# Seven block products in place of eight for the feed-forward value chunks, and a down projection in three parts

## The chip, the cores and the metric

The kernel runs on one core of a Trainium2 chip. The metric is the device time of one execution in microseconds, the median of several runs. Five engines work at once, each through its own queue in the order in which the program wrote it: TensorE (PE, matrix products), VectorE (DVE), ScalarE (ACT), GpSimd (POOL) and SyncE (SP, which only starts transfers here). They wait for each other through semaphores.

## The reference, cut to what matters

Two blocks run one after the other on 512 tokens of width 1024. The first block has two layers, and each layer ends in the feed-forward part that is changed here:

```python
def conv_ffn(x, w_up, conv_w, conv_b, w_down):          # x: 512 x 1024, D_FF = 2816
    a, g = jnp.split(x @ w_up, 2, axis=-1)              # value half a, gate half g
    g = lax.conv_general_dilated(g, conv_w[:, None, :].astype(g.dtype), window_strides=(1,),
                                 padding=((CONV_W - 1, 0),), ..., feature_group_count=D_FF) + conv_b
    return (jax.nn.gelu(g) * a) @ w_down                # three-tap causal convolution per channel
```

The result is added to the residual and a layer norm follows. After the second layer an RMS norm for the next block follows as well.

## The kernel before, in words

All arithmetic is float32 to within rounding, by splitting. An operand is cut into a high part (a cast to the matmul's reduced format, on ACT, line 238 for weights and 371 for activations) and a low part (operand minus high part, on DVE at line 242 or POOL at 240, and 372). A product is then three matmuls: high x high, low x high, high x low (`mm3`, lines 276 to 278). The activations `xh`, `xl` lie transposed, 128 partitions x 8 slices of the width x 512 tokens.

The up projection works on chunks of 128 columns of D_FF, 22 gate chunks and 22 value chunks. A weight transfer (`unit`) of 1 MB brings the columns of two chunks into one of two `raw` buffers; each chunk is a `piece` that is split into a high and a low tile. `get` gives back the tiles of the piece just used and calls `pump`, which starts the next transfer if a `raw` buffer is free and issues the next split, up to five pieces ahead. So the splits of later pieces stand in ACT's and DVE's queues where `get` was called.

The order is two gate chunks, then the two value chunks that belong to them (a pair, 11 pairs in a layer). `fms` runs a chunk as 24 matmuls of 512 columns (8 slices x 3) into one PSUM bank (`fm`), then calls its evacuation. `g_evac` (line 1134) does the convolution and the gelu: ACT (1137), DVE twice (1138, 1139), ACT (1140). `a_evac` (1143) multiplies the value chunk from PSUM with the gate (DVE, 1145) and splits the product for the down projection. The first pair of a layer runs in two halves of 256 tokens (`split=SPL`), since the norm before it delivers the tokens in four tiles.

The chunks are taken in parts of 12 and 10 (`FF_PARTS`, line 1101). After each part the down projection (`tm`) multiplies its chunks with their rows of `w_down` in two halves of 512 output columns. The first part is added to the residual (`residual`, 405); the last goes through `out_proj`, whose last half works tile by tile of 128 tokens (`tail=5` pieces held at once), followed by each tile's layer norm (lines 403 to 425), the transposes (391) for the next stage, and in the second layer the RMS norm (443 to 451). `norm_params`, and in the second layer `lru_params` (some 30 very small DVE steps and an exponential on ACT), are issued after the first part's chunks.

Of the kernel before, what the change touches and what calls it, by code (L numbers as in the profile page):

```python
# [12 lines left out]
F32R = mybir.dt.float32r  # L13
# [15 lines left out]
SPL = 4  # L29
# [84 lines left out]
class Core:  # L114
# [4 lines left out]
    def __init__(self, ctx, tc, io):  # L119
# [17 lines left out]
        self.live = deque()  # L137
        self.nm = 0
# [37 lines left out]
    def piece(self, u, view, a, b, direct=False):  # L176
        self.units[u]["left"] += 1
        self.plist.append((u, view, a, b, direct))

    def pump(self, split=True):  # L180
        while True:
# [14 lines left out]
            if split and n < len(self.plist) and self.room():  # L196
                u, view, a, b, direct = self.plist[n]
                raw = self.units[u]["tile"]
                if raw is not None:
# [3 lines left out]
                    else:  # L203
                        self.live.append((None,) + self.split_piece(src, a, b))
                        self.units[u]["left"] -= 1
                    self.next_piece += 1
# [45 lines left out]
    held = 0  # L252

    def get(self, n=1):
# [11 lines left out]
        self.pump()  # L266
# [6 lines left out]
    def mm3(self, out, lhs, rhs, start, stop):  # L273
        (lh, ll), (rh, rl) = lhs, rhs
        mm = self.T.matmul
        mm(out, lh, rh, start=start, stop=False)  # L276
        mm(out, lh, rl, start=False, stop=False)  # L277
        mm(out, ll, rh, start=False, stop=stop)  # L278
# [12 lines left out]
    def fms(self, evacs, split=0):  # L291
# [3 lines left out]
        if split:  # L295
            self.flush(1)
            self.extra, self.eager = 0, False
            ws = self.get(split)
            pss = [self.ps() for _ in ws]
            for t0 in (0, 256):  # L300
                for k, (w, p) in enumerate(zip(ws, pss)):
                    if t0 or k == split - 1:
                        self.flush(3 if t0 else 2)
                    yield from self.fm(p, w, t0=t0, t1=t0 + 256)
                    if t0:
                        evacs[k](p)
                        if k == EAGER:
# [3 lines left out]
        for f in evacs[n:]:  # L311
# [3 lines left out]
            f(p)  # L315

# [784 lines left out]
    FF_PARTS = (12, 10)  # L1101

    def ffn_weights(self, l):
        w = self.io["ffn_w_up"][l].rearrange("(k p) n -> p k n", p=128)
        c = 0
        for part in self.FF_PARTS:
            for j in range(c, c + part, 2):
                for base in (D_FF, 0):
                    u = self.unit([(lambda r: r.rearrange("p (k n) -> p k n", k=8), w[:, :, base + 128 * j:base + 128 * j + 256])])
                    for q in range(2):  # L1110
# [16 lines left out]
    def ffn(self, l, rms=False):  # L1127
        A, V, al, fr = self.A, self.V, self.al, self.fr
# [14 lines left out]
        def a_evac(c, p):  # L1143
            acc = H[c]
            V.tensor_tensor(acc, p, acc, op=MUL)  # L1145
            hi, lo = al(F32R), al(F32R)
# [4 lines left out]
        for part in self.FF_PARTS:  # L1151
            fs = []
            for j in range(c0, c0 + part, 2):
                fs += [lambda p, c=c: g_evac(c, p) for c in (j, j + 1)] + [lambda p, c=c: a_evac(c, p) for c in (j, j + 1)]
            run(self.fms(fs, split=SPL if c0 == 0 else 0))
            if c0 == 0:
                gb = self.norm_params(l, 1)
                if rms:
# [977 lines left out]
```

## Time and profile before

| | us |
|---|---|
| time, median of 3 runs (2002.7 to 2004.19) | 2003.87 |
| the profiled execution's own time | 1997.43 |
| its span, first to last instruction | 1995.5 |
| PE busy with matmuls | 1947.4 (98%) |
| DVE busy | 991.2 (50%) |
| ACT busy | 817.5 (41%) |
| POOL busy | 417.6 (21%) |

All times in the rows are from the one profiled execution. Matmuls are pipelined: a matmul's own duration is longer than the distance to the next one, so their cost is read from the distance between two starts. The feed-forward part of the first layer starts at about 300 us and its last matmul is followed by the next stage's first at 665 us; the second layer's lies between about 964 and 1331 us.

### The profile page before, as it was taken

The numbers are of one execution on the slowest core, as the hardware profiler recorded it, in microseconds if no ns is written. First come the engines' busy times: TensorE is split into PE (matmuls) and PEld (weight loads), VectorE is DVE, ScalarE is ACT, GpSimd is POOL, SyncE is SP. The second block draws the span as 40 slices with busy tenths as digits, with TensorE's granted clock in tenths as the row PEclk, the third lists the DMA queues.
The fourth block names the chain that finished last, engine by engine and source line by source line (L and its number), as shares of the span: only waits on it lengthen the run. The fifth ranks groups of instructions, "written<-read, shape, count | busy, mean of one in ns | idle before, by whom it ended". The sixth has DMA issues, their size and how long they took to land.

```text
span 1995.5 us, 25737 instructions
## 1 busy us (share of the span) xinstructions
PE 1947.4 (98%) x10228; PEld 1623.8 (81%) x10228; DVE 991.2 (50%) x1692; ACT 817.5 (41%) x1451; POOL 417.6 (21%) x368
## 2 busy tenths in 40 slices
PE   8999989999999999999999999999998999999998
PEld 6678868888888988777888888888886888888887
DVE  3553255442444533763655344375667555455443
ACT  3455434331333344784333233256655533333331
POOL 0334441000000264474300000031443211011000
PEclk9999999999999999999999999999999999999999
DMA  6432223232323433111232423232231322222221
GB/s 199 112 115 68 93 84 101 95 127 85 105 85 123 137 99 122 54 49 64 65 116 94 137 85 105 85 106 70 71 89 70 133 85 90 90 85 90 85 75 52
DMA packets 174164, 189.22 MB, mean 95 GB/s; under 512 B 15080, under 2 KB 133662, under 8 KB 174045
## 3 DMA queue, kind: packets, MB, share of 16 engines
q1 hardware_dynamic: 158044, 165.63, 26.2%
q10 hardware_dynamic: 12064, 17.37, 2.9%
q0 software_dynamic: 3936, 4.59, 0.7%
q8 instruction: 80, 1.31, 0.3%
q14 instruction: 40, 0.32, 0.0%
HBM read 182.19 MB, written 6.65 MB: 95 GB/s over the span
## 4 chain that ended last, share of the span: by engine, by line
PE 80%; DVE 8%; ACT 3%; issue 2%; SPq 2%; DMA 2%; POOL 2%; ACTq 0%; DVEq 0%; POOLq 0%
PE p L276 24%; PE p L277 24%; PE p L278 24%; SPq L190 1%; PE p L1545 1%; PE p L1525 1%; PE p L1663 1%; SPq L851 1%; DVE s L1891 1%; POOL lo L240 1%; PE p L391 1%; PE p L786 1%; DVE s L1890 1%; PE p L366 1%; ACT hi L238 0%
## 5 line engine op out<-in xcount | busy, mean ns | idle before, releaser
L276 PE MATMUL p<-xh,hi 128*128 128x512 f32 (+1 forms) x1200 | 457.9, 382 | 0.7 <-ACT xh L371 0.7
L238 ACT CAST hi<-raw 128x1024 fp32r<-128x1024 f32 (+4 forms) x294 | 301.4, 1033 | 382.5 <-PE p L278 307.9
L277 PE MATMUL p<-xl,hi 128*128 128x512 f32 (+1 forms) x1200 | 454.3, 379 | 1.3 <-DVE xl L372 1.3
L278 PE MATMUL p<-xh,lo 128*128 128x512 f32 (+1 forms) x1200 | 454.3, 379 | 0.4 <-DVE lo L242 0.4
L242 DVE TENSOR_TENSOR lo<-raw,hi 128x1024 fp32r<-128x1024 f32 (+2 forms) x212 | 258.7, 1227 | 356.3 <-ACT hi L238 336.8
L276 PE MATMUL p<-hi,s 128*128 128x512 f32 (+1 forms) x728 | 285.7, 392 | 7.5 <-ACT s L371 4.8
L278 PE MATMUL p<-hi,s 128*128 128x512 f32 (+1 forms) x728 | 283.6, 390 | 0.0
L277 PE MATMUL p<-lo,s 128*128 128x512 f32 (+1 forms) x728 | 282.9, 389 | 0.0
L276 PEld LDWEIGHTS p<-xh,hi 128*128 128x128 f32 x1200 | 225.9, 188 | 44.7 <-ACT xh L371 1.4
L278 PEld LDWEIGHTS p<-xh,lo 128*128 128x128 f32 x1200 | 226.0, 188 | 43.1 <-DVE lo L242 0.6
L277 PEld LDWEIGHTS p<-xl,hi 128*128 128x128 f32 x1200 | 226.0, 188 | 42.8 <-DVE xl L372 2.1
L240 POOL TENSOR_TENSOR lo<-raw,hi 128x1024 fp32r<-128x1024 f32 (+3 forms) x82 | 191.2, 2339 | 329.2 <-ACT hi L238 259.6
L422 POOL TENSOR_TENSOR xtok<-xtok,b 128x512 f32<-128x512 f32 x16 | 26.1, 1629 | 712.9 <-ACT xtok L421 371.9
L276 PE MATMUL p<-hi,xh 128*128 128x512 f32 (+3 forms) x480 | 170.1, 354 | 1.5 <-ACT s L841 0.8
L277 PE MATMUL p<-lo,xh 128*128 128x512 f32 (+3 forms) x480 | 169.0, 352 | 0.5 <-DVE lo L242 0.5
L278 PE MATMUL p<-hi,xl 128*128 128x512 f32 (+3 forms) x480 | 168.8, 352 | 0.0
L276 PEld LDWEIGHTS p<-hi,s 128*128 128x128 f32 x728 | 137.1, 188 | 36.9 <-ACT s L371 6.2
L371 ACT CAST s<-s 128x512 fp32r<-128x512 f32 (+1 forms) x100 | 59.1, 597 | 260.8 <-DVE s L1145 122.7
L278 PEld LDWEIGHTS p<-hi,s 128*128 128x128 f32 x728 | 137.1, 188 | 30.0 <-DVE s L372 2.1
L277 PEld LDWEIGHTS p<-lo,s 128*128 128x128 f32 x728 | 137.1, 188 | 26.6
L276 PEld LDWEIGHTS p<-hi,xh 128*128 128x128 f32 x480 | 90.6, 189 | 14.3 <-issue 1.7
L277 PEld LDWEIGHTS p<-lo,xh 128*128 128x128 f32 x480 | 90.6, 189 | 11.7 <-DVE lo L242 0.8
(313 smaller groups left out, 2584.9 us busy)
## 6 DMA issues: line engine op xcount, KB each, us to landing
raw<-in_ffn_w_up_dram SPq DMA_DIRECT2D x44, 1024.0 KB, 5.1
raw<-in_ret_w_in_dram SPq DMA_DIRECT2D x24, 1024.0 KB, 5.1
raw<-in_ffn_w_down_dram SPq DMA_DIRECT2D x20, 1024.0 KB, 5.1
raw<-in_ev_w_in_dram SPq DMA_DIRECT2D x24, 512.0 KB, 5.3
raw<-in_lru_w_in_dram SPq DMA_DIRECT2D x24, 512.0 KB, 5.7
raw<-in_ret_w_out_dram SPq DMA_DIRECT2D x8, 1024.0 KB, 5.0
raw<-in_lru_w_out_dram SPq DMA_DIRECT2D x6, 1024.0 KB, 5.0
s<-in_od_cmp_w_dram ACTq DMA_DIRECT2D x16, 256.0 KB, 4.8
```

Of the source, the lines that this page charges most:

```text
L190: self.nc.sync.dma_start(dst(raw), src)
L238: self.A.copy(dh, x)
L240: self.G.tensor_tensor(dl, x, dh, op=SUB)
L242: self.V.tensor_tensor(dl, x, dh, op=SUB)
L276: mm(out, lh, rh, start=start, stop=False)
L277: mm(out, lh, rl, start=False, stop=False)
L278: mm(out, ll, rh, start=False, stop=stop)
L366: self.T.matmul(outs[e][:, :n], q[a][r, i * 128:i * 128 + 128], k[b][r, :n], start=j == 0, stop=j == 2)
L371: self.A.copy(hi, src)
L391: self.T.transpose(p[:, c * 128:(c + 1) * 128], halves[b][:, c * 128:(c + 1) * 128], self.ident)
L422: self.G.tensor_tensor(b, b, gb[0][:, 512:], op=MUL)
L786: T.matmul(o[:, i * 128:i * 128 + 128], st["pt"][:, k * 128:k * 128 + 128], va[k][:, h * 128:h * 128 + 128], start=k == 0, stop=k == i)
```

## The change: what it does

Only the value chunks of the pairs 2 to 11 in both layers change their arithmetic. For a pair the 1024 x 256 weight block is seen as 2 x 2 blocks: b11, b12, b21, b22, the first index the half of the width (four slices), the second the chunk. The activations are seen likewise as a11, a12 (first 256 tokens, two halves of the width) and a21, a22 (last 256 tokens). Eight block products become seven (Winograd's form of Strassen's algorithm), with

- sums of activations, once a layer: s1 = a21 + a22, s2 = s1 - a11, s3 = a11 - a21, s4 = a12 - s2, each split again (`sum_steps`; eight splits, held in 16 slots for the layer);
- sums of weights, four POOL instructions for each pair, in place in `raw` (`seven`): T1 = b12 - b11, T3 = b22 - b12, T2 = b22 - T1, and b21 - T2. A pair has three pieces, V0 (b11, b21), V1 (T1, b21 - T2) and V2 (T3, T2), and the split of b22 (`corner`);
- `fm7`: seven products of 12 matmuls of 256 columns in the order P1 to P7 of this document: P1 = b11 a11 into bank x, P2 = b21 a12 into z, P3 = T2 s2 added on top of x, P4 = T1 s1 into y, P5 = T3 s3 on top of x, P6 = (b21 - T2) a22 into e, P7 = b22 s4 on top of y. Between them ACT copies x to SBUF three times (before P3, P5 and after P5) and DVE makes five sums of 256 columns; `a_evac` reads the result from SBUF.

The parts become 6, 8 and 8 chunks; the first two are added to the residual, the last holds 4 pieces in its tail. `norm_params` and `lru_params` are issued after the first pair.

```diff
+    def seven(self, u):
+        v = lambda r: r.rearrange("p (k n) -> p k n", k=8)
+        def post(r):
+            w = v(r)
+            b11, b12, b21, b22 = w[:, :4, :128], w[:, :4, 128:], w[:, 4:, :128], w[:, 4:, 128:]
+            h, l = self.al(F32R), self.al(F32R)
+            self.split(h.rearrange("p (k n) -> p k n", k=4), l.rearrange("p (k n) -> p k n", k=4), b22)
+            self.corner.append((h, l))
+            self.G.tensor_tensor(b11, b12, b11, op=SUB)
+            self.G.tensor_tensor(b12, b22, b12, op=SUB)
+            self.G.tensor_tensor(b22, b22, b11, op=SUB)
+            self.G.tensor_tensor(b21, b21, b22, op=SUB)
+        for c, f in ((0, post), (0, None), (128, None)):
+            self.piece(u, lambda r, c=c: v(r)[:, :, c:c + 128], 8, 128, post=f)
...
+                        if post is not None:
+                            post(raw)
+                            self.cool, most = 1, 0
...
-        self.pump()
+        if self.cool and len(self.live) >= n:
+            self.cool, most = 0, 0
+        self.pump(most=max(most, n - len(self.live)))
...
+    def sum_steps(self, early):
...
+        def part(n):
+            hs, ls = [al(F32R), al(F32R)], [al(F32R), al(F32R)]
+            for h, l, t in zip(hs, ls, self.qs[n]):
+                self.split(h, l, t)
+            self.sums[n] = hs, ls
+        if early:
+            return [lambda: whole(G, "a11", 0, 0), lambda: whole(G, "a12", 0, 1)]
+        return [lambda: whole(G, "a21", 1, 0), lambda: whole(V, "a22", 1, 1),
+                lambda: comb(V, "s1", "a21", "a22", ADD, "a22"), lambda: comb(G, "s3", "a11", "a21", SUB, "a21"),
+                lambda: part("s1"), lambda: comb(G, "s2", "s1", "a11", SUB, "a11"), lambda: fr(*self.qs.pop("s1")),
+                lambda: part("s2"), lambda: comb(G, "s4", "a12", "s2", SUB, "a12"), lambda: fr(*self.qs.pop("s2")),
+                lambda: part("s3"), lambda: fr(*self.qs.pop("s3")), lambda: part("s4"), lambda: fr(*self.qs.pop("s4"))]
...
+    def fm7(self, evacs):
...
+        def mm(p, b, x, start=True):
+            for k in range(4):
+                self.mm3(p[:, :256], (b[0](k), b[1](k)), x(k), start and k == 0, k == 3, on=not start)
+            return 12 * 120
...
+        w, = self.get(most=1)
+        x, z, y, e = (self.ps() for _ in range(4))
+        t0, t1 = self.al(), self.al()
+        yield mm(x, blk(w, 0), a(0, 0))
+        A.copy(t0[:, :256], x[:, :256])
+        yield mm(z, blk(w, 1), a(0, 1))
+        V.tensor_tensor(t0[:, :256], t0[:, :256], z[:, :256], op=ADD)
+        w, v = self.get(2, most=1)
+        self.cool = 0
+        yield mm(x, blk(v, 1), s("s2"), False)
+        A.copy(t1[:, :256], x[:, :256])
+        yield mm(y, blk(w, 0), s("s1"))
+        yield mm(x, blk(v, 0), s("s3"), False)
+        A.copy(t0[:, 256:], x[:, :256])
+        V.tensor_tensor(t1[:, 256:], t0[:, 256:], y[:, :256], op=ADD)
+        yield mm(e, blk(w, 1), a(1, 1))
+        V.tensor_tensor(t0[:, 256:], t0[:, 256:], e[:, :256], op=ADD)
+        evacs[0](t0)
+        corner = self.corner.popleft()
+        yield mm(y, [lambda k, t=t: t[:, 128 * k:128 * k + 128] for t in corner], s("s4"), False)
+        self.fr(*corner)
+        V.tensor_tensor(t1[:, :256], t1[:, :256], y[:, :256], op=ADD)
+        evacs[1](t1)
...
-    FF_PARTS = (12, 10)
+    FF_PARTS = (6, 8, 8)
...
+                gs = [lambda p, c=c: g_evac(c, p) for c in (j, j + 1)]
+                if j == 0:
+                    run(self.fms(gs + [lambda p, c=c: a_evac(c, p) for c in (j, j + 1)], split=SPL, sums=True))
+                    gb = self.norm_params(l, 1)
+                    if rms:
+                        g = self.bcast(self.io["norm_pre_2"][0])
+                        self.lru_params()
...
+                    continue
+                for _ in self.fms(gs):
+                    self.steps(4)
+                run(self.fm7([lambda p, c=c: a_evac(c, p, True) for c in (j, j + 1)]))
```

Where the change puts ACT's work: in the first layer, a pair in the middle of a part, before. A row is the line, the operation, out<-in by the program's names, the shape, and which engines' semaphores it waits for.

```order
L1137 ACTIVATE s_3346<-p_3321,par 128x512 [waits PE_49]
L1140 ACTIVATE s_3346<-s_3346 128x512 [waits DVE_49,Activation_49]
L238 CAST hi_3351<-raw_3215 128x1024
L1137 ACTIVATE s_3382<-p_3357,par 128x512 [waits PE_49]
L1140 ACTIVATE s_3382<-s_3382 128x512 [waits DVE_49,Activation_49]
L238 CAST hi_3387<-raw_3285 128x1024 [waits DMAHW0_49]
L371 CAST s_3417<-s_3346 128x512 [waits DVE_49]
L238 CAST hi_3421<-raw_3285 128x1024 [waits PE_49]
L371 CAST s_3453<-s_3382 128x512 [waits DVE_49]
L238 CAST hi_3457<-raw_3355 128x1024 [waits DMAHW1_49,PE_49]
```

The same place on ACT now (lines of the changed kernel: 1271 and 1274 are the gate's two ACT steps, 263 a weight split, 502 an activation's or the corner's split, 428, 434 and 437 the copies of bank x).

```order
L1271 ACTIVATE s_4124<-p_4099,par 128x512 [waits PE_49]
L1274 ACTIVATE s_4124<-s_4124 128x512 [waits DVE_49,Activation_49]
L263 CAST hi_4129<-raw_3968 128x1024 [waits DMAHW1_49]
L1271 ACTIVATE s_4158<-p_4133,par 128x512 [waits PE_49]
L1274 ACTIVATE s_4158<-s_4158 128x512 [waits DVE_49,Activation_49]
L263 CAST hi_4163<-raw_3968 128x1024
L428 COPY s_4173<-p_4169 128x256 [waits PE_49]
L263 CAST hi_4201<-raw_4097 128x1024 [waits DMAHW2_49,PE_49]
L502 CAST s_4205<-raw_4097 128x512
L434 COPY s_4174<-p_4169 128x256 [waits PE_49]
L437 COPY s_4173<-p_4169 128x256 [waits PE_49]
```

The copies are new; the first of them stands behind the second gate's gelu and a weight split. PE at the same place: the last matmul of P2, then P3, and the first of P4 and P5. Bank x is p_4169, the sums s2 are s_3040 and s_3042.

```order
L307 MATMUL p_4170<-xh_2587,lo_4003 128x256
L305 MATMUL p_4169<-s_3040,hi_4093 128x256 [waits Activation_49]
L306 MATMUL p_4169<-s_3042,hi_4093 128x256
L307 MATMUL p_4169<-s_3040,lo_4094 128x256 [waits DVE_49]
...
L305 MATMUL p_4171<-s_3001,hi_4089 128x256
...
L305 MATMUL p_4169<-s_3079,hi_4093 128x256 [waits Activation_49]
```

Before, PE went from one chunk to the next there with no wait in a matmul:

```order
L276 MATMUL p_3357<-xh_2587,hi_3211 128x512
L277 MATMUL p_3357<-xl_2588,hi_3211 128x512
L278 MATMUL p_3357<-xh_2587,lo_3212 128x512
L276 MATMUL p_3392<-xh_2587,hi_3351 128x512
L277 MATMUL p_3392<-xl_2588,hi_3351 128x512
```

POOL at the start of the first layer's feed-forward part, from the last norm before it. Before, only a transfer followed:

```order
L422 TENSOR_TENSOR xtok<-xtok,b_2248 128x512 [waits Activation_49]
L423 TENSOR_TENSOR xtok<-xtok,b_2250 128x512 [waits Pool_49]
L531 DMA scr_3741<-flat 512x1x640
L422 TENSOR_TENSOR xtok<-xtok,b_3737 128x512 [waits DMAHW7_49,PE_49,Activation_49]
L423 TENSOR_TENSOR xtok<-xtok,b_3739 128x512 [waits DMAHW0_49,Pool_49]
```

Now the sums stand there (374 and 379), and the first pair's four weight sums (193 to 196) stand ahead of s2 and s4, the last four rows. Rows of a11, a12 and the other halves of a21 and s3 are left out.

```order
L554 TENSOR_TENSOR xtok<-xtok,b_2250 128x512 [waits Pool_49]
...
L374 TENSOR_TENSOR s_2913<-xh_2587,xl_2588 128x512 [waits DVE_49]
...
L379 TENSOR_TENSOR s_2914<-s_2774,s_2914 128x512 [waits DVE_49]
L193 TENSOR_TENSOR raw_2615<-raw_2615 128x4x128 [waits DMAHW2_49,DVE_49]
L194 TENSOR_TENSOR raw_2615<-raw_2615 128x4x128 [waits Pool_49]
L195 TENSOR_TENSOR raw_2615<-raw_2615 128x4x128 [waits DVE_49,Pool_49]
L196 TENSOR_TENSOR raw_2615<-raw_2615 128x4x128 [waits Pool_49]
L379 TENSOR_TENSOR s_2773<-s_2917,s_2773 128x512
L379 TENSOR_TENSOR s_2774<-s_2918,s_2774 128x512
L379 TENSOR_TENSOR s_2777<-s_2777,s_2773 128x512 [waits Pool_49]
L379 TENSOR_TENSOR s_2778<-s_2778,s_2774 128x512 [waits Pool_49]
```

All of s1 to s4 must pass through these rows, and through ACT and DVE, before the first pair's last product.

## Rows read from the trace of the kernel before

**Rows 1.** The page: span, busy times, granted clock in 40 slices.
```profile
span 1995.5 us, 25737 instructions
PE 1947.4 (98%) x10228; PEld 1623.8 (81%) x10228; DVE 991.2 (50%) x1692; ACT 817.5 (41%) x1451; POOL 417.6 (21%) x368
PEclk9999999999999999999999999999999999999999
```

**Rows 2.** PE's waits in 297 to 650 us: total, times, longest.
```profile
PE p L391 <- POOL xtok L423: 1.8, 1, 1.8
PE p L277 <- DVE xl L372: 0.3, 1, 0.3
PE p L276 <- ACT xh L371: 0.2, 1, 0.2
```

**Rows 3.** Timeline of PE: start and duration in us, engine, line, operation, shapes.
```profile
302.02 0.28 PE L276 MATMUL p<-xh,hi 128*128 128x256 f32 x1
304.90 0.28 PE L276 MATMUL p<-xh,hi 128*128 128x256 f32 x1
...
358.76 0.39 PE L276 MATMUL p<-xh,hi 128*128 128x512 f32 x1
```

**Rows 4.** Timeline of ACT and DVE at that second gate chunk's evacuation.
```profile
358.97 0.78 ACT L1137 ACTIVATE s<-p,par 128x512 f32<-128x512 f32 x1 [1.43 <-PE p L278]
361.41 0.63 ACT L1140 ACTIVATE s<-s 128x512 f32<-128x512 f32 x1 [1.66 <-DVE s L1139]
361.94 1.04 ACT L238 CAST hi<-raw 128x1024 fp32r<-128x1024 f32 x1
...
359.78 0.75 DVE L1138 SCALAR_TENSOR_TENSOR s<-p,par,s 128x511 f32<-128x511 f32 x1 [0.98 <-ACT s L1137]
```

**Rows 5.** Lines with steps from PSUM: count, ns min/median/max, first and last start, shapes.
```profile
L985 ACT COPY s<-p x8: 373/586/591, 255.8 to 274.7; 128x512 f32<-128x512 f32 x6, 128x256 f32<-128x256 f32 x2
L1995 DVE TENSOR_TENSOR s<-p,s x16: 284/485/692, 1635.0 to 1867.8; 128x512 f32<-128x512 f32 x4, 128x384 f32<-128x384 f32 x4, 128x256 f32<-128x256 f32 x4, 128x128 f32<-128x128 f32 x4
```

**Rows 6.** Lines of splits and of POOL's steps: ns min/median/max.
```profile
L371 ACT CAST s<-s x100: 300/622/628, 327.4 to 1868.1; 128x512 fp32r<-128x512 f32 x88, 128x384 fp32r<-128x384 f32 x4, 128x256 fp32r<-128x256 f32 x4, 128x128 fp32r<-128x128 f32 x4
L242 DVE TENSOR_TENSOR lo<-raw,hi x212: 1001/1226/1859, 8.3 to 1962.9; 128x1024 fp32r<-128x1024 f32 x103, 128x816 fp32r<-128x816 f32 x2, 128x896 fp32r<-128x896 f32 x1
L422 POOL TENSOR_TENSOR xtok<-xtok,b x16: 1281/1668/1751, 288.5 to 1333.5; 128x512 f32<-128x512 f32 x16
```

**Rows 7.** Timeline of POOL and DVE, 283 to 291 us.
```profile
283.45 5.04 POOL L240 TENSOR_TENSOR s<-raw,s 128x512 fp32r<-128x512 f32 x4
290.26 1.63 POOL L423 TENSOR_TENSOR xtok<-xtok,b 128x512 f32<-128x512 f32 x1
...
287.18 1.86 DVE L424 SCALAR_TENSOR_TENSOR xtok<-xtok,mv,b 128x512 f32<-128x512 f32 x1
290.66 0.67 DVE L405 SCALAR_TENSOR_TENSOR xtok<-xtok,p 128x512 f32<-128x512 f32 x1
```

**Rows 8.** Timeline, start of the first layer's feed-forward part: DVE, ACT, PE.
```profile
313.87 1.29 DVE L372 TENSOR_TENSOR xl<-p,xh 128x512 fp32r<-128x512 f32 x2 [2.46 <-ACT xh L371]
...
326.89 0.64 ACT L1140 ACTIVATE s<-s 128x512 f32<-128x512 f32 x1 [2.31 <-DVE s L1139]
...
326.10 0.40 PE L276 MATMUL p<-xh,hi 128*128 128x512 f32 x1
```

**Rows 9.** Timeline of DVE and ACT, second layer: first and last of `lru_params`, a transfer before it.
```profile
1101.08 0.17 DVE L1794 TENSOR_SCALAR hb<-par 128x24 f32<-128x24 f32 x1
1107.68 0.17 DVE L1813 TENSOR_SCALAR sp<-sp 128x12 f32<-128x12 f32 x1
...
1099.82 0.34 ACTq L430 DMA_DIRECT2D b<-in_ln_g_dram  x1
1101.15 1.28 ACT L1799 ACT_TABLE_LOAD   x1 [0.71 <-issue]
```

**Rows 10.** Timeline of PE at the second layer's end.
```profile
1329.69 0.66 PE L391 MATMUL p<-ident,s 128*128 128x128 f32 x4 [0.82 <-POOL s L450]
```

More of the change, by code (lines that the diff above doesn't have):

```diff
@@ L137, in __init__ @@
         self.live = deque()
+        self.corner = deque()
+        self.todo = deque()
         self.nm = 0
@@ L195, in pump @@
             n = self.next_piece
-            if split and n < len(self.plist) and self.room():
-                u, view, a, b, direct = self.plist[n]
+            if split and most and n < len(self.plist) and self.room():
+                u, view, a, b, direct, post = self.plist[n]
                 raw = self.units[u]["tile"]
@@ L252, with get @@
     held = 0
-    def get(self, n=1):
+    cool = 0
+    def get(self, n=1, most=1000):
         for _ in range(self.held):
@@ L289, in fm, with fms @@
                 yield self.step * 3 * 216 * (t1 - t0) // 512
-    def fms(self, evacs, split=0):
+    def fms(self, evacs, split=0, sums=False):
         n = 0
@@ L296, in fms @@
             self.flush(1)
+            if sums:
+                self.todo.extend(self.sum_steps(True))
+                self.steps()
             self.extra, self.eager = 0, False
@@ L303, in fms @@
                         self.flush(3 if t0 else 2)
+                    if t0 and k == 0 and sums:
+                        self.todo.extend(self.sum_steps(False))
+                        self.steps(4)
                     yield from self.fm(p, w, t0=t0, t1=t0 + 256)
@@ L306, in fms @@
                         evacs[k](p)
+                        if k:
+                            self.steps(3)
                         if k == EAGER:
@@ new lines, in steps, with fr_sums, a, s @@
+    def steps(self, n=1000):
+        while n and self.todo:
+            self.todo.popleft()()
+            n -= 1
+    def fr_sums(self):
+        for hs, ls in self.sums.values():
+            self.fr(*hs, *ls)
+    def fm7(self, evacs):
+        V, A = self.V, self.A
+        def a(th, kh):
+            return lambda k: (self.quarter(self.xh, th, kh)[:, k], self.quarter(self.xl, th, kh)[:, k])
+        def s(n):
+            hs, ls = self.sums[n]
+            return lambda k: tuple(t[k // 2][:, 256 * (k % 2):256 * (k % 2) + 256] for t in (hs, ls))
+        def mm(p, b, x, start=True):
+            for k in range(4):
+                self.mm3(p[:, :256], (b[0](k), b[1](k)), x(k), start and k == 0, k == 3, on=not start)
+            return 12 * 120
+        def blk(w, r):
+            return [lambda k, t=t: t[:, 4 * r + k] for t in w]
+        w, = self.get(most=1)
[21 more added lines that the diff above has]
+        evacs[1](t1)
```

62 lines of the change are left out of this document (39 added, 23 removed).

## The prediction

> **What bounds the kernel now.** First the page's busy times: PE computes for 1947.4 of 1995.5 us, at the full granted clock in every slice, and no other engine is over 50% [rows 1]. Then PE's list of waits over the first layer's feed-forward part: 2.3 us in 353, all of them at its start, around the transposes and the first tiles [rows 2]. So PE's stream of matmuls sets the time there, and whatever makes it shorter is a gain as long as nothing else makes PE wait. Then the timeline of PE, for the price of a matmul: from 326.10 to 358.76 us stand six chunks of 24 matmuls of 512 columns [rows 3, 8], 32.66 / 144 = 0.2268 us each; between 302.02 and 304.90 stand 24 of 256 columns [rows 3], 0.120 us each. Half the columns cost 53% of the time, not 50%. Last the timelines of ACT and DVE, for how long an evacuation takes: a gate chunk's first ACT step starts 0.21 us after PE's next chunk, and it, two DVE steps, the gelu and the weight split that stands behind them end at 361.94 + 1.04 = 362.98, so 4.22 us after the chunk's end on PE at 358.76 [rows 3, 4]. Before, nobody waited for that: PE was computing the two value chunks in other banks.
>
> **The columns saved.** A pair of value chunks was 48 matmuls of 512 columns, 48 x 0.2268 = 10.89 us. It becomes 84 of 256 columns, 84 x 0.120 = 10.08. That is 0.81 us for a pair, and 20 pairs in the two layers: -16.2 us. Gates and the down projection keep their matmuls.
>
> The row says 13 to 14 us above the columns' own time in each matmul of either size. The Trainium skill, "TensorE: Matmul & The Clock Gate", section "Wait — 56ns, not 53.3ns?", has only about 2.5 ns there at the full clock; by it the seven products would save about 1.2 us a pair and 24 in all. The rows differ from it in this kernel, so they decide.
>
> **The new wait inside each pair.** P3 adds on top of bank x, so PE must wait until ACT has copied P1 out of it. PE reaches P3 after P1 and P2, 24 x 0.120 = 2.88 us after the second gate chunk. In ACT's queue that copy stands behind this gate chunk's first step, its gelu and one weight split, in the order that I showed; these three are unchanged, so they end 4.22 us after the chunk as before. The copy of 128 x 256 from PSUM takes 0.37 [rows 5]. 4.22 + 0.37 - 2.88 = 1.71 us in which PE stands still; with about 0.1 less for the overlap of ACT's steps and as much for the signal, I keep 1.7. It is twice what the pair saves. Queued behind the waiting P3 is all of PE's later work.
>
> The other waits in the pair just fit. After P3 starts, at 4.6 us from the gate's end, ACT splits the next V0 and its corner (1.05 + 0.62) and copies x again after P3's end at 6.1; P5 wants it at 7.5. The third copy starts 0.21 after P5's end at 8.9, 0.37 [rows 5], then a DVE sum with one PSUM operand, between 0.28 and 0.49 by the shapes of its row [rows 5], so about 9.9; P7 wants it after P6, at 10.4. DVE and ACT have in a pair of 22.7 us about 14 and 11 us of work by the durations of rows 4 to 6, so they keep up on the average. POOL's four weight sums, 1.28 to 1.75 each [rows 6], begin when V0 is split and are done by about 14 us, 3 us into the next pair's first gate chunk; V1 and V2 are split behind them, a pair ahead of their use. I cost them at nothing because of that lead; without it they are the third rival.
>
> What POOL's sums do to DVE is the place where a rule speaks. A DVE step with two SBUF operands took 1.86 us beside POOL's splits, while one with a PSUM operand took its usual 0.67 beside a POOL step [rows 7]. That is what the Trainium skill has in "SBUF — State Buffer", section "Who interferes with whom": with two SBUF inputs, the later of the two blocks until the first has finished. By it the DVE sum ahead of P7, with one operand in PSUM, stays free, and the splits and the sums of activations below do not; the trace agrees. If every DVE step blocked, P7 would wait up to a POOL step longer in each pair.
>
> 18 of the 20 pairs go like this: 18 x 1.7 = +30.6 us. Bounds: 1.4 (all overlaps in favour) and 2.2 (P7 half a microsecond late as well), 25 to 40 us.
>
> **The first pair in each layer.** It must have all four sums of activations, split. I place them by rows from the first layer. The last tile's low part is ready at 313.87 + 1.29 = 315.2 [rows 8]. POOL's a21 follows, 2 x 1.28; DVE's s1 waits for it in front of the first gate's evacuation. That and the corner's split on ACT make the second gate's gelu, 326.89 before [rows 8], about 2 us later. From 329 ACT has eight splits of sums and two of value chunks at 0.62 [rows 6], 6.2 us; two transfers to start, about 0.4 each [rows 9]; then for the pair's own first gate 0.78 + 2 x 0.75 + 0.63 [rows 4], three weight splits, 3.1, the second gate and its split, about 4, and the copy. With no wait anywhere this is 329 + 17.5 = 346.5. PE would have started P3 at 326.10 + 10.88 + 2.88 = 339.9 [rows 3, 8]: a stall of 6.6, the lower end. POOL adds waits: its weight sums, s2 and s4 are eight steps in a row from about 326.7, which end between 337 (1.28 each) and 340.7 (1.75 each) [rows 6], and s4's two splits on ACT can't come earlier. After them stand 1.2 + 0.8 + 3 + 3.1 + 1.2 (DVE's third low part, for which the second gate's steps wait) + 4 + 0.4 less 0.4 overlap, 13.3 us: P3 at 350 to 354, a stall of 10 to 14. I take 12 in the first layer, as this chain has a row for each link.
>
> In the second layer `lru_params` now stands in front of the first gate's evacuation. On DVE it took 1101.08 to 1107.85, 6.8 us, and an exponential's table load 1.28 on ACT [rows 9], where before the down projection covered it; the gelu's table must be loaded again, 1.28 more. Some of it lies beside ACT's splits. I add 7: 19 us, bounds 12 and 23. Both layers +31, bounds 19 to 37.
>
> **The rest.** Three parts instead of two bring eight more additions of 0.67 on DVE [rows 7] in each layer, while PE multiplies from other banks: nothing. Before, PE did not wait at the change from chunks to down projection or back [rows 2], and down-projection pieces are still split ahead there: nothing, 1 us at the most. The last tail has 24 matmuls for a tile in place of 30, 5.4 us and not 6.8, so the transposes of the first two tiles come 2.7 us sooner after their sums. In the second layer PE already waited there, 0.82 us [rows 10]; I add 2, bounds 0 and 3.
>
> **Sum.** -16.2 + 30.6 + 31 + 2 = +47.4 us. The profiled execution took 1997.43, which would become 2044.8; it lies 6.4 below the median of the runs, so the forecast is 2003.87 + 47.4 = 2051 us.
>
> **Rivals.**
> *Only the wait in the pair.* If the sums of activations pass beside the first pair, or most of it, each first pair costs 1.7 as the others: -16.2 + 34 + 2 = +20, 2024 us. For it: DVE and ACT are under 60% busy. Against: their queues are in order, and ten splits stand in front of the evacuation.
> *Faster.* The price of the seven products is one stall per pair, ahead of P3, and it decides at 0.81 us: below that the pair gains. That is so if ACT's copy is done 3.7 us after the second gate's end. With the weight split moved away it would be 3.6. If that split and the copy ran inside P2, and the sums beside the first pair, the time would be 2003.9 - 16.2 + 2 = 1990. For it: PE is the bound and gets less work. Against: the split stands ahead of the copy in the program, and the row gives 4.22 to its end.
> *POOL comes onto the path.* Its four steps run among DVE's splits, and both stop each other. If V1 and V2 or the sum ahead of P7 come one POOL step late in each pair, 1.3 x 20 = 26 more: 2077. For it: the row of 1.86 us. Against: a lead of several microseconds.
>
> **How the numbers follow.** Forecast 0.62, the first rival 0.14, the second 0.08, the third 0.12, and 0.04 for something between the first two that leaves the time where it was. The bounds of the terms reach from 2003.87 - 16.2 + 25 + 19 + 0 = 2032 to 2003.87 - 16.2 + 40 + 37 + 3 = 2068. To hold eight in ten the range takes most of the first and some of the third rival: 2022 to 2076. A measurement of this kernel can tell 0.2%, 4 us, from no change. Faster by more: 0.08; within: 0.04; slower by more: 0.88.
>
> **What would show it.** In the profile of the changed kernel PE's list of waits has a row of some 20 waits of P3's first matmul on ACT's copy (line 428), about 1.7 us each, with two of 10 us or more; the chain of waits passes through the second gate's gelu. P5's and P7's first matmuls wait little. The distance between P1's matmuls is 0.120. PE's busy time falls by some 16 us. The forecast is wrong if the copy is reached sooner than 3.7 us after the gate, if the first pairs stall by less than 5 us, or if the waits on POOL are long in every pair.

## The result and the profile after

The changed kernel takes 2063.5 us (median of 4 runs, 2062.3 to 2065.9), the kernel before 2003.6 us beside it: 59.9 us slower, ratio 1.0301 with an interval of 1.0283 to 1.0319. The forecast was 2051, within 2022 to 2076. The profiled run of after lies at its median and that of before 6 us below its own, so the two profiles differ by 66.7 us; the differences between stretches below are those of the profiles.

The page of after, against [rows 1]: span, busy times, PE's busy share and granted clock in 40 slices.

```profile
span 2062.4 us, 27637 instructions
PE 1949.2 (95%) x10948; PEld 1656.6 (80%) x10948; DVE 1099.7 (53%) x1852; ACT 873.5 (42%) x1567; POOL 567.0 (27%) x472
PE   8999897999999999999959999999999999999998
PEclk9999999999999999999989999999999999999999
```

PE has the same busy time in a longer span; the slices of the two first seven-product pairs have 7 and 5, and the second of them a clock digit of 8. PE's list of waits (total, times, longest) over the first layer's feed-forward, 297 to 690 us, against [rows 2]:

```profile
PE p L305 <- ACT s L428: 25.6, 10, 12.1
PE p L305 <- ACT s L434: 4.6, 1, 4.6
...
PE p L305 <- DVE s L1279: 1.3, 1, 1.3
```

and over the second layer's, 960 to 1400 us:

```profile
PE p L305 <- ACT s L428: 32.6, 10, 19.1
PE p L522 <- POOL s L581: 2.4, 2, 1.7
```

L428 is the copy of P1 ahead of P3, and it is waited for in all 20 pairs: 18 times 1.50 us, once 12.1 and once 19.1. L434 is the copy of P3 ahead of P5. L1279 reads the bank into which P2 goes, in the second layer too. By the start of each stretch's first matmul, the first feed-forward is 29.9 us longer, the second 32.5, and the three stretches before, between and behind them 1.5 each.

A steady pair in after: PE's last matmul of P2 and first of P3, then ACT from the second gate chunk's evacuation on (against [rows 4]).

```profile
462.31 0.28 PE L307 MATMUL p<-xh,lo 128*128 128x256 f32 x1
464.08 0.39 PE L305 MATMUL p<-s,hi 128*128 128x256 f32 x1 [1.50 <-ACT s L428]
...
459.76 0.78 ACT L1271 ACTIVATE s<-p,par 128x512 f32<-128x512 f32 x1 [1.05 <-PE p L307]
462.19 0.63 ACT L1274 ACTIVATE s<-s 128x512 f32<-128x512 f32 x1 [1.66 <-DVE s L1273]
462.73 1.03 ACT L263 CAST hi<-raw 128x1024 fp32r<-128x1024 f32 x1
463.67 0.36 ACT L428 COPY s<-p 128x256 f32<-128x256 f32 x1
```

ACT has P1 to copy from 461.2 on, and copies at 463.67, behind the gelu and the split. The bracket counts from the modelled end of the matmul before; from start to start PE loses 464.08 - 462.31 - 0.12 = 1.65 us.

The first seven-product pairs, PE in the first layer and in the second:

```profile
341.46 0.39 PE L305 MATMUL p<-xh,hi 128*128 128x256 f32 x1 [1.32 <-DVE s L1279]
355.25 0.58 PE L305 MATMUL p<-s,hi 128*128 128x256 f32 x1 [12.09 <-ACT s L428]
364.30 0.58 PE L305 MATMUL p<-s,hi 128*128 128x256 f32 x1 [4.60 <-ACT s L434]
...
1057.60 0.58 PE L305 MATMUL p<-s,hi 128*128 128x256 f32 x1 [19.15 <-ACT s L428]
```

and behind these waits PE's windows: length, busy time, granted clock, transfers.

```profile
355.20:358.00 2.80, 2.75 (x13) 0.50 0.74 161
...
370.00:374.00 4.00, 4.00 (x22) 1.00 0.02 4
1057.50:1061.00 3.50, 3.40 (x16) 0.50 0.28 72
```

A granted clock of 0.50 is 1.2 GHz of 2.4. In the first of these windows the matmuls of 256 columns stand 0.213 us apart and not 0.120.

The wait of 4.60 follows a transfer. The chain of waits of after, in order of time (start, length, what):

```profile
350.76 11.57 DMA raw<-in_ffn_w_up_dram
...
362.41 1.04 ACT hi L263
363.45 0.52 ACT s L502
363.97 0.28 ACT s L434
```

The copy ahead of P5 stands in ACT's queue behind the split of the next pair's V0, and V0's weights took 11.57 us to land, beside the table's transfer (issued at 340.20).

### The profile page after: what moved, and what is told of

Its sections match the earlier page's. It is cut to its first block, busy times and chain, and to the rows that moved or that the text cites. A ratio compares the mean times of both kernels' runs of the same rounds, so it can differ in the third digit from the quotient of the medians.

```text
span 2062.4 us, 27637 instructions
## 1 busy us (share of the span) xinstructions
PE 1949.2 (95%) x10948; PEld 1656.6 (80%) x10948; DVE 1099.7 (53%) x1852; ACT 873.5 (42%) x1567; POOL 567.0 (27%) x472
## 4 chain that ended last, share of the span: by engine, by line
PE 74%; DVE 12%; ACT 7%; issue 3%; DMA 2%; SPq 1%; POOL 1%; ACTq 0%; DVEq 0%; POOLq 0%
PE p L305 22%; PE p L306 22%; PE p L307 22%; ACT hi L263 2%; DVE s L503 1%; PE p L1686 1%; PE p L1666 1%; PE p L1804 1%; DVE s L1273 1%; DVE s L2032 1%; DVE s L1272 1%; DMA raw<-in_ffn_w_up_dram 1%; SPq L211 1%; DVE s L2031 1%; ACT s L1271 1%
## 5 line engine op out<-in xcount | busy, mean ns | idle before, releaser
L263 ACT CAST hi<-raw 128x1024 fp32r<-128x1024 f32 (+4 forms) x314 | 319.6, 1031 | 380.5 <-PE p L307 254.5
L267 DVE TENSOR_TENSOR lo<-raw,hi 128x1024 fp32r<-128x1024 f32 (+2 forms) x232 | 281.0, 1225 | 320.5 <-ACT hi L263 300.5
L305 PE MATMUL p<-xh,hi 128*128 128x512 f32 (+1 forms) x1120 | 403.3, 360 | 4.4 <-DVE s L1279 2.6
L306 PE MATMUL p<-xl,hi 128*128 128x512 f32 (+1 forms) x1120 | 399.7, 357 | 2.1 <-DVE xl L503 2.0
L307 PE MATMUL p<-xh,lo 128*128 128x512 f32 (+1 forms) x1120 | 398.8, 356 | 0.0
L306 PEld LDWEIGHTS p<-xl,hi 128*128 128x128 f32 x1120 | 213.4, 191 | 32.1 <-DVE xl L503 3.6
L307 PEld LDWEIGHTS p<-xh,lo 128*128 128x128 f32 x1120 | 213.3, 190 | 30.1
L193 POOL TENSOR_TENSOR raw<-raw 128x512 f32<-128x512 f32 x20 | 32.6, 1630 | 480.6 <-DVE lo L267 480.6
L305 PE MATMUL p<-s,hi 128*128 128x256 f32 (+1 forms) x296 | 94.1, 318 | 62.9 <-ACT s L428 58.2
L503 DVE TENSOR_TENSOR s<-s,s 128x512 fp32r<-128x512 f32 (+1 forms) x116 | 94.6, 831 | 59.2 <-ACT s L502 58.0
```

Source lines behind the costliest of these rows:

```text
L193: self.G.tensor_tensor(b11, b12, b11, op=SUB)
L263: self.A.copy(dh, x)
L267: self.V.tensor_tensor(dl, x, dh, op=SUB)
L305: mm(out, lh, rh, start=start, stop=False, skip_group_check=on)
L306: mm(out, lh, rl, start=False, stop=False, skip_group_check=on)
L307: mm(out, ll, rh, start=False, stop=stop, skip_group_check=on)
```

## The experiments

My theory: the 60 us are ACT's and DVE's queue order, a copy waiting behind work that PE doesn't need yet. Against it stood two rivals: the seven products and their evacuations don't fit beside PE at all, or the loss lies in the parts, the sums or the parameters. Ratios are to the kernel before.

**The next split behind P1's copy** (split_later).

```diff
-        w, = self.get(most=1)
+        w, = self.get(most=-1)
...
         A.copy(t0[:, :256], x[:, :256])
+        self.pump(most=1)
```

With -1, `get` calls no `pump` unless the piece that it must give back isn't split yet.

> The first copy of bank x is issued ahead of the weight split that stood before it on ScalarE; all else is the changed kernel. Theory (P3 waits for that copy, which waits in ScalarE's order): the copy ends about 1 us sooner, the wait ahead of P3 falls from 1.66 us (start to start) to about 0.7 in all pairs, a part of it comes back ahead of P5, since the split then stands before the second copy: 13 to 19 us less than 2063.5, about 2047. Rival (P3 waits for the sums or the splits of V2, or for an engine's throughput): no change, 2061 to 2066.

2045.4 us, 1.021 [1.0195, 1.0225]: 18.1 less than after. As the theory had it. The steady wait is

```profile
461.80 0.39 PE L306 MATMUL p<-s,hi 128*128 128x256 f32 x1 [0.55 <-ACT s L429]
```

and now the gelu stands just ahead of the copy.

**The parameters behind the first part** (params_later).

```diff
-                    gb = self.norm_params(l, 1)
-                    if rms:
...
+            if c0 == 0:
+                gb = self.norm_params(l, 1)
+                if rms:
+                    g = self.bcast(self.io["norm_pre_2"][0])
+                    self.lru_params()
+                if l == 0 and self.pre_rms:
+                    self.table(4)
```

> The norm's parameters, lru_params and the table transfer are issued after the first part's chunks again, as before the change; all else is the changed kernel. Theory: the long wait of the second layer's first pair falls from 19 us to about 12, as in the first layer, and the 4.6 us wait ahead of P5 in the first layer goes, with the half clock after it, since the table transfer no longer runs beside the weight transfer: 13 us less, about 2050. Rival (both waits come from the sums and the late start of the weight transfer alone): 2060 to 2065, the 4.6 us wait stays.

2051.5 us, 1.0243 [1.0226, 1.0260]: 12.0 less. The second layer's long wait fell from 19.1 to 12.1, as in the first, and the wait at P5 went. The run moves the norm's parameters too, but the first layer has those as well, and there P3's wait stays at 12.1; so the 7 us belong to `lru_params`. In after its steps hold DVE from 1040.4 to 1046.3, ahead of the gate's taps, and the gelu then loads its table for 1.28.

**The table's transfer alone** (table_later).

```diff
-                    if l == 0 and self.pre_rms:
-                        self.table(4)
...
+            if c0 == 0 and l == 0 and self.pre_rms:
+                self.table(4)
             c0 += part
```

> The changed kernel with the transfer of the table alone issued behind the first part of the first feed-forward; the norm and LRU parameters stay where they are. Theory (P5's 4.6 us in the first feed-forward come from V0's weights landing late beside the table's transfer, and nothing else): that wait falls below 0.5 us and the half-clock stretch behind it shortens, P1's copy is still waited for 12 us in the first feed-forward and 19 us in the second, the sum 5 to 7 us under the changed kernel, some 2057 us. Rival (the backlog of sums on ScalarE and VectorE makes that wait too): it stays above 3 us, 2062 us or more.

2059.4 us, 1.0287 [1.0272, 1.0303]: 4.1 less, a little under what was expected. The wait at P5 is gone, the other two stay at 12.1 and 19.1. The transfer made that wait.

**The second pair with eight products** (second_pair_plain).

```diff
-                    if j and base == 0:
+                    if j > 2 and base == 0:
...
+                if j == 2:
+                    for _ in self.fms(gs + [lambda p, c=c: a_evac(c, p) for c in (j, j + 1)]):
+                        self.steps(4)
```

> The second pair of each layer keeps eight products, so seven products begin with the third pair; all else is the changed kernel. Theory (the long waits are the sums' way through POOL, DVE and ACT, and the sums are done a pair later): both long waits, the 4.6 us one and the half clock after them go, some 41 us, and 1.6 us of columns are lost: about 2024. Rival (the backlog in the queues only moves on): a wait of 5 us or more shows in the second or third pair, and the time stays above 2035.

2046.4 us, 1.021 [1.0195, 1.0225]: 17 less, far from 2024. P3 of the first seven-product pair still waited 8.2 us in both layers, at half the clock afterwards. But it was not the sums of activations: the chain of waits in the first layer is

```profile
341.26 9.77 DMA raw<-in_ffn_w_up_dram
...
353.44 1.67 POOL raw L193
...
358.25 1.30 POOL raw L196
359.58 1.06 ACT hi L263
```

POOL's four weight sums take 359.58 - 353.44 = 6.1 us, V1 and V2 are split only behind them, and those splits stand ahead of the gates' evacuation. In the second layer the chain passes through the same four steps. The lead of a pair that hides them elsewhere does not exist yet at the first seven-product pair, and there the prediction's third rival was true.

**P6 ahead of P3, P7 in a bank of its own** (p6_first).

```diff
         yield mm(z, blk(w, 1), a(0, 1))
         V.tensor_tensor(t0[:, :256], t0[:, :256], z[:, :256], op=ADD)
         w, v = self.get(2, most=1)
         self.cool = 0
+        yield mm(e, blk(w, 1), a(1, 1))
...
-        yield mm(y, [lambda k, t=t: t[:, 128 * k:128 * k + 128] for t in corner], s("s4"), False)
+        yield mm(q, [lambda k, t=t: t[:, 128 * k:128 * k + 128] for t in corner], s("s4"))
```

> P6 is computed ahead of P3, and P7 goes to a bank of its own with one more sum of 256 columns on VectorE; all else is the changed kernel. Theory: PE has 36 matmuls and not 24 between the second gate and P3, 1.44 us more cover, so the wait ahead of P3 falls to about 0.2 us in 18 pairs and by 1.44 in the two first ones: 27 to 29 us less, about 2035. Rival (the wait is not one for a copy of fixed length): less than 10 us gained, or the wait turns up ahead of P5 or P7.

2048.6 us, 1.0226 [1.0210, 1.0241]: 15 less and not 28. A product more ahead of P3 should hide nearly all of the copy, yet in 13 of the 18 steady pairs the wait is 0.59 to 0.78 (in the other five P3 starts 0.22 late):

```profile
460.36 0.63 ACT L1275 ACTIVATE s<-s 128x512 f32<-128x512 f32 x1 [2.12 <-DVE s L1274]
460.89 1.03 ACT L263 CAST hi<-raw 128x1024 fp32r<-128x1024 f32 x1
461.83 0.36 ACT L428 COPY s<-p 128x256 f32<-128x256 f32 x1
```

PE's gate chunk ended at 457.00, and the copy came 4.83 us later, 0.7 more than in after: DVE's taps, for which the gelu waits, came later. A chain through two queues has no fixed length. In the first pairs 5.2 and 12.2 us of the long waits now stand ahead of P6, which waits for a weight split.

**The parts alone** (parts_only; on the kernel before).

```diff
-    FF_PARTS = (12, 10)
+    FF_PARTS = (6, 8, 8)
...
```

The first two parts go to the residual, and the last one's tail holds 4 pieces, as in the changed kernel.

> The kernel before with its down projection in parts of 6, 8, 8 and nothing else. Theory (the loss is the seven-product pairs' waits, the parts cost next to nothing): 2003.5 to 2006.5 us, both feed-forwards within 1.5 us of their length before. Rival (the third part costs its own fill and drain): each feed-forward 4 us or more longer, 2012 us or more.

2003.6 us, 1.0009 [0.9998, 1.0019], no change. The first feed-forward keeps its length to 0.1 us, the second is 1.95 longer, a little over the 1.5 expected, 1.6 of it PE waiting for the last tiles' norm (L450: 2.4 us, 0.8 before).

**The gelu behind the copy as well** (gelu_later; on split_later).

```diff
-            A.activation(acc, acc, AF.Gelu_apprx_tanh)
+            self.late.append(lambda: A.activation(acc, acc, AF.Gelu_apprx_tanh))
+            if not (c % 2 and c > 1):
+                self.late.pop()()
...
         A.copy(t0[:, :256], x[:, :256])
+        self.late.pop()()
```

> As split_later, and besides the second gate's Gelu stands behind the copy of P1 in ScalarE's order, not ahead of it. Theory (the 0.55 us that split_later's 18 steady pairs still wait is the copy standing behind a Gelu that waits for VectorE's taps, not the copy's own length): the steady wait is 0.1 us or less, 18 x (0.55 + 0.16) = 12.8 us less than split_later, some 2033 us; the long waits of the first pairs (11, 5 and 18 us) stay. Rival (the split that P3 needs then ends last, or the copy itself): the steady wait stays above 0.4 us with another releaser, 2043 us or more.

2034.0 us, 1.0161 [1.0141, 1.0181]: 11.4 less than split_later. None of the 18 steady pairs waits at P3. The list of waits puts the long ones into the first pairs:

```profile
PE p L306 <- ACT s L429: 23.1, 2, 15.1
PE p L306 <- ACT s L437: 10.1, 2, 7.9
```

In the first layer 12.1 + 4.6 has become 8.0 + 7.9: P5 started at 363.98, in after at 364.30, since its copy still waited for the transfer. Twelve of the 18 steady pairs now lose 0.34 at P5, which the list doesn't show; late_start tells why.

**Seven products from the second part on** (late_start; the edits of gelu_later, the parameters and the table behind the first part's down projection, and the sums spread over the pairs 2 and 3, two steps behind each chunk).

```diff
-                    if j and base == 0:
+                    if j >= 6 and base == 0:
...
-                for _ in self.fms(gs):
-                    self.steps(4)
+                if j < 6:
+                    for n, f in enumerate(gs + [lambda p, c=c: a_evac(c, p) for c in (j, j + 1)]):
+                        run(self.fms([f]))
+                        self.steps(2)
+                    continue
+                run(self.fms(gs))
```

> As gelu_later, with the norm, LRU and table parameters issued behind the first part, and seven products only from the second part on (16 of 22 pairs): the two further pairs of the first part have eight products, and the fourteen steps that form the sums, with the two early ones, are spread over those two pairs, two steps behind each of their eight chunks, none in the first pair. Theory (the waits are all of order and none of the products themselves): no wait for P1's copy over 0.3 us, no stretch of a feed-forward at half the granted clock behind such a wait, each seven-product pair 0.8 us shorter than eight products, 16 x 0.81 = 13 us less than parts_only, so 1990 to 1997 us. Rival (ScalarE and VectorE can't take the sums and splits beside a pair's own work anywhere, the backlog only moves): waits of several us in the pairs with two steps a chunk or in the first seven-product pair, 2004 us or more.

2000.3 us, 0.9989 [0.9981, 0.9998]. The waits of 4.6 us and more are gone; the longest left is 2.0, at P5 of the second layer's first seven-product pair. But only 3.3 of the expected 13 us against parts_only are there. The list of waits doesn't tell why. A pair, ACT and PE:

```profile
441.37 1.98 ACT L263 CAST hi<-raw 128x1024 fp32r<-128x1024 f32 x2
443.26 0.61 ACT L497 CAST s<-raw 128x512 fp32r<-128x512 f32 x1
443.78 0.36 ACT L429 COPY s<-p 128x256 f32<-128x256 f32 x1
...
443.82 0.28 PE L308 MATMUL p<-s,lo 128*128 128x256 f32 x1
444.19 0.38 PE L306 MATMUL p<-s,hi 128*128 128x256 f32 x1
```

P5's first matmul starts 0.37 after the last of P4 and its second 0.23 later, where 0.12 is usual: 0.35 lost. No bracket shows it, since it is hidden in the modelled end of 0.28. The copy of P3 stood behind the splits of V0 and its corner. Nine of the 16 pairs lose that, one 0.6, the first seven-product pairs of the two layers 1.6 and 4.4, and four nothing.

**V0's split behind P3's copy, parameters ahead of the first part's down projection** (mended; otherwise late_start).

```diff
-        w, v = self.get(2, most=1)
-        self.cool = 0
+        w, v = self.get(2, most=-1)
...
         A.copy(t1[:, :256], x[:, :256])
+        self.cool = 0
+        self.pump(most=1)
```

> As late_start, with two orders more: the split of the next weight piece that stands ahead of the copy of P3 in ScalarE's order, with the corner's split, goes behind it, and the norm, LRU and table parameters are issued ahead of the first part's down projection, not behind it. Theory (late_start's seven-product pairs lie 0.46 us below eight products and not 0.79, since P5 starts 0.34 us late behind those splits, which the profile doesn't count as a wait, and its first seven pairs lose 1.2 and some 4 us to parameters and the table's transfer): the three products on s take 4.32 us in every pair, the first seven pairs lose under 1 us, 16 x 0.79 = 12.6 us less than parts_only with 1 to 3 us left over in first pairs and ends: 1991 to 1995 us. Rival (the splits that move back then make the next pair's gates wait): 1998 us or more, with new waits for weight pieces at the gates.

1999.9 us, 0.9988 [0.9980, 0.9997]: missed. The first pairs lose nothing any more, P5 is nearly cured (0.06 to 0.08 in most pairs), but eight of the sixteen P7 start 0.5 to 0.9 late and four more 0.24:

```profile
441.15 0.41 DVE L434 TENSOR_TENSOR s<-s,p 128x256 f32<-128x256 f32 x1
...
441.62 0.39 PE L306 MATMUL p<-s,s 128*128 128x256 f32 x1 [0.65 <-DVE s L434]
```

L434 is the sum that empties P4's bank for P7, behind DVE's half of the same splits.

**The same split behind that sum too** (mended_again).

```diff
         A.copy(t1[:, :256], x[:, :256])
-        self.cool = 0
-        self.pump(most=1)
...
         V.tensor_tensor(t1[:, 256:], t0[:, 256:], y[:, :256], op=ADD)
+        self.cool = 0
+        self.pump(most=1)
```

> As mended, with the split of the next value piece and of its corner moved once more, behind VectorE's sum of P4's bank (mended's P7 started 0.8 us late in 8 pairs, because that sum, which empties the bank that P7 goes on top of, stood behind these splits). Theory (only orders on the two in-order engines were left): the wait at P7 goes, all seven products of a pair take 10.1 us in every pair, and the sum is 16 x 0.79 = 12.6 us under parts_only less 2 us at the ends of the feed-forwards: 1990 to 1994 us. Rival (VectorE has no free time in a pair and each move sends the wait on): new waits at the next pair's gates or at its P1, 1998 us or more.

2001.0 us, 0.9994 [0.9985, 1.0003]: missed again. P7 is cured, and P5 loses 0.8 in 12 pairs:

```profile
443.46 0.63 ACT L1271 ACTIVATE s<-s 128x512 f32<-128x512 f32 x1 [2.24 <-DVE s L1270]
444.00 1.03 ACT L263 CAST hi<-raw 128x1024 fp32r<-128x1024 f32 x1
444.94 0.36 ACT L428 COPY s<-p 128x256 f32<-128x256 f32 x1
```

Twice now the rival, by which each move only sends the wait on, was right.

**Gelu and split behind P3's copy** (both_copies_first; otherwise mended_again).

```diff
         A.copy(t0[:, :256], x[:, :256])
-        self.late.pop()()
-        self.pump(most=1)
...
         A.copy(t1[:, :256], x[:, :256])
+        self.late.pop()()
+        self.pump(most=1)
```

> As mended_again, with the second gate's Gelu and the split behind it moved behind the copy of P3 as well (mended_again's P5 started 0.8 us late in 12 pairs: the Gelu waited for VectorE's taps, which stood behind three splits, and the copy of P3 stood behind Gelu and split). Theory (the wait at P5 is again order alone, and VectorE has 1.4 us of room before the next product that asks for it): P5 starts without a wait, all seven products take 10.1 us in every pair, 12 x 0.79 = 9.5 us under mended_again's feed-forwards: 1990 to 1994 us. Rival (VectorE is the bound inside a pair, and the wait moves to P7's bank, P1 or the next gates): 1998 us or more, as the three versions before it.

1989.0 us (1988.3 to 1990.7), 0.9932 [0.9919, 0.9946]: faster than the kernel before. A pair of it: the first matmuls of P1 and of the next gate chunk on PE, then ACT.

```profile
437.05 0.28 PE L306 MATMUL p<-xh,hi 128*128 128x256 f32 x1
...
447.13 0.40 PE L306 MATMUL p<-xh,hi 128*128 128x512 f32 x1
...
439.03 0.36 ACT L421 COPY s<-p 128x256 f32<-128x256 f32 x1
441.57 0.37 ACT L426 COPY s<-p 128x256 f32<-128x256 f32 x1 [2.18 <-PE p L308]
441.83 0.64 ACT L1271 ACTIVATE s<-s 128x512 f32<-128x512 f32 x1
444.45 0.37 ACT L431 COPY s<-p 128x256 f32<-128x256 f32 x1 [1.04 <-PE p L308]
```

Each copy follows its product, and the gelu stands behind the two that PE waits for. The pair takes 447.13 - 437.05 = 10.08 us, 84 x 0.120: no gap is left, in any of the 16 pairs. The feed-forwards are 6.2 and 6.3 us shorter than with parts_only, 16 x 0.79 = 12.6, which is the whole saving in columns.

**The orders without the late start** (orders_only; the orders of mended_again, the sums where the changed kernel has them).

```diff
-                    if j >= 6 and base == 0:
+                    if j and base == 0:
```

> The same orders as mended_again and the parameters ahead of the first part's down projection, but seven products from the second pair on, with the sums where the changed kernel has them. Theory (what is left is then the backlog of sums alone, at the two first pairs, with the half-clock stretch behind it): steady pairs wait for nothing, 18 x 0.79 = 14 us under parts_only, and the two first pairs cost 12 to 16 us each with their banks, long waits and half clock: 2013 to 2021 us, that is 20 to 30 us over mended_again. Rival (the backlog costs little once the orders are right): under 2005 us.

2020.5 us, 1.0090 [1.0074, 1.0105], 19.5 us over mended_again: the time that the theory gave, but not with steady pairs that wait for nothing. Fourteen of the 18 lose 0.8 ahead of P5, as twelve of mended_again's 16 do. In the two first pairs P3 waited 8.0 us, P2 1.3, and a granted clock of 0.50 followed. Here the chain does pass through the sums, which DVE splits two and three in a row ahead of the first pair's evacuations.

## Why the prediction was right, and where it was not

- *Columns, -16.2.* Right. P1's matmuls stand 0.120 apart, and both_copies_first has the 0.79 in each pair. The 13 to 14 that the prediction sets above the columns' own time are ns and not us; the sum doesn't use them.
- *The wait in the pair, 18 x 1.7 = 30.6.* Right in place, cause and size: 1.65 each, 29.7. The chain passes through gate, taps, gelu, split and copy. split_later and gelu_later show that it is their order: 18.1 and 11.4 us came back, together 29.5, although twelve pairs then lose 0.34 at P5.
- *P5 and P7 just fit.* They do in after's steady pairs: from P4 on, each product starts 1.44 behind the one before. What the stall at P3 costs besides its 1.65 is 0.10 at P3's second matmul, which starts 0.22 behind the first and not 0.12. The stall also gives ACT and DVE 1.65 us in each pair. Where it was taken away P5 or P7 no longer fitted, until both copies stood first; the prediction hadn't seen that one wait pays for the other two.
- *The first pairs, 12 and 19.* Right to 0.3 us: 12.25 and 19.3 from start to start. The 7 us for `lru_params` are shown by params_later. The 12 was partly luck: it was counted along POOL's eight steps, which end at 340.26 as forecast (337 to 340.7), but in after the chain of waits passes them by. It goes through DVE's splits of the sums, two, three and five in a row (from 331.02, 335.74 and 342.09), and through the two value evacuations between them. P2 and P3 together wait 13.7. Missed beside them: P2's bank, since DVE's splits of sums stand ahead of the evacuation of the first pair (1.5 in each layer, 3 in all); the transfer of the table beside V0's (4.8 at P5); and the clock.

```profile
333.87 6.39 POOL L379 TENSOR_TENSOR s<-s,s 128x512 f32<-128x512 f32 x4
...
335.74 5.06 DVE L503 TENSOR_TENSOR s<-s,s 128x512 fp32r<-128x512 f32 x3 [0.69 <-ACT s L502]
340.73 0.68 DVE L1279 TENSOR_TENSOR s<-p,s 128x512 f32<-128x512 f32 x1
342.09 2.50 DVE L503 TENSOR_TENSOR s<-s,s 128x512 fp32r<-128x512 f32 x4 [0.68 <-ACT s L502]
```

This is POOL and DVE ahead of P2's bank in the first layer: three splits on DVE took 5.06 us, 1.69 each, beside POOL's sums, and four 2.50, 0.63 each, when POOL was done. It is the blocking of two SBUF operands that the prediction weighed by [rows 7]; its price was known there and put neither on this place nor on the way to P3.

The price of the clock stood in the trace of before as well: a wait of PE and the window behind it, in which matmuls of 512 columns stand 0.43 apart and not 0.23. The page's slices of 50 us are too coarse to show it.

```profile
1509.90 0.56 PE L276 MATMUL p<-hi,s 128*128 128x512 f32 x1 [2.18 <-DVE s L1848]
...
1510.30:1513.50 3.20, 3.20 (x9) 0.50 0.06 24
```

- *The rest, 2.* The longer wait of the tail is there (1.6 by the list of waits, with parts_only as well); the slower clock at the start of the next stage, whose first 72 matmuls took 11.8 us and 9.3 before, is not in the sum.
- *PE's busy time falls by 16.* Wrong: 1949.2 and 1947.4. A busy time sums modelled durations, in which a matmul at the lower clock counts 0.41 and not 0.28, and the last matmul before each stall counts 0.28 where a followed one adds 0.12. In both_copies_first, without the stalls, it is 1939.8, and 1953.1 in parts_only: there the columns saved do show.
- *Rivals.* Of the faster one the point of decision was right (0.81 us at P3), and even its place: with the split behind the copy (split_later) a steady pair takes 10.87, as long as eight products (10.89), and with the gelu behind it too it gains. Its 1990 was reached by both_copies_first, though not with the sums in the first pair. POOL came onto the path in no steady pair, but at the start of second_pair_plain.

What the sum lacked lies almost all in the first pairs: P2's bank, the table's transfer and the clock behind the long waits. Terms as measured, within the two feed-forwards of the profiles: -16 + 29.7 + 31.5 + 3 (P2) + 4.8 (P5) + 1.8 (P3's second matmul, 0.10 in each of 18 pairs) + some 5 (the clock) + 1.6 (tail) = 61, against 29.9 + 32.5 = 62.4. The forecast's 47.4 lies 12.5 below the medians' 59.9, and P2, P5 and the clock are as much.

## What to carry to other kernels

When a product is added on top of a bank that must first be copied out, the copy is on PE's path: issue it ahead of everything in its queue that isn't needed sooner, the evacuation of the chunk before included. A saving of a few per cent of PE's columns, here 0.79 us of 21.8 in a pair, can be smaller than one step out of order in an ACT or DVE queue (1.65), so compare distances between starts, pair by pair, and not the list of waits alone. Set up sums of activations where eight plain products still run, and keep parameters and other transfers out of the first pair.

## What the runs showed of the hardware

- After PE had waited 8 us or more in these pairs, the granted clock was 0.50 for the first matmuls behind the wait: 12 of them at 0.213 us after the 12.1, some 18 after the 4.6 that came 9 us later. Shorter waits were followed by it too: 2.18 in before, and 2.03 in late_start (0.50 from 1086.7 to 1088.7). In orders_only the window behind 8.0 us reads

```profile
347.40:349.40 2.00, 2.00 (x9) 0.50 0.62 201
```

  while behind the 1.5 us waits of after's steady pairs it stayed at 1.00. Why the next stage of after also starts at 0.50, behind waits of only 1.71 and 0.59, no run here settles; parts_only has the same two waits there and stays at 1.00.
- A 1 MB weight transfer took 11.6 us to land beside the table's 1280 KB (5.2 is the page's median for these transfers), and PE waited for it through a copy that has nothing to do with these weights.
- The same work can be free in one order and cost most of a saving in another. In both_copies_first a pair's window (length, busy time of PE, its weight loads, DVE, ACT and POOL, clock, transfers) is

```profile
430.00:451.50 21.50, 21.50 (x136) 19.50 (x135) 15.96 (x21) 10.00 (x15) 7.00 (x5) 1.00 0.30 99
```

  DVE has 5.5 us to spare and ACT 11.5, and yet three other orders of the same work lost 9 to 10 of the 12.6 us again (late_start, mended and mended_again, by the pairs' starts).
